# Hymba block on one Trainium2 core: x brought in transposed, first V taken from raw columns, row sums of squares by matmuls with ones

## The chip, the cores and the metric

The kernel runs on one core of one Trainium2 chip. The metric is the device time of one execution in microseconds; the median of several runs is compared. Engines are named as in the profile: PE is TensorE's matmul, PEld its weight load, DVE VectorE, ACT ScalarE, POOL GpSimd, SP the engine that issues most DMAs.

## The reference

One encoder block in fp32 over two requests, a prompt of 512 tokens and a sample of 1024, of width 1024; the kernel treats them as 12 blocks of 128 tokens, or 3 chunks of 512.

```python
xn = rmsnorm(h, norm_mix_g)              # h * rsqrt(mean(h*h) + 1e-6) * g
z = xn @ w_in                            # 3072 columns: q, k, v, g_att, u, g_f of 512 each
att = diff_attention(q, k, v, lam, rel_bias)
att = rmsnorm(att, subln_g, SUBLN_EPS) * (1.0 - lambda_init)
att = att * silu(g_att)
fno = fourier_mix(u, w_f) * silu(g_f)
h = h + concatenate([att, fno]) @ w_out
gate = sigmoid(rmsnorm(h, ple_norm_g) @ w_ple_gate)
h = h + gate * (p_i @ w_ple_proj)
y = rmsnorm(h, final_norm_g)
```

## The kernel before, in words

Every fp32 product is made of three matmuls on two reduced parts: `split` writes a high part (a cast, mostly on ACT, L55) and a low part (source minus high part, mostly on DVE, L59), and `mm3` (L66, L67, L68) adds high*high, high*low and low*high into one PSUM bank. A token block times 512 columns of a weight is 8 k-blocks of three, 24 matmuls.

The stages follow each other on PE:

- **V.** `load_nat(1024)` brings columns 1024 to 1535 of `w_in` in four loads of 512 KB (tile `raw`, pool `pn`, four buffers) and splits them into `wnh`, `wnl`. `prep(t)` takes a block of 128 token rows: Square with a row sum on ACT (L272), mean on DVE, power on POOL (L276), scaled by the row's factor and by `gmix` (the mix weights spread over all partitions) on DVE (L277), eight transposes on PE (L284), and splits into `xh`, `xl`, which hold the normed x transposed, for all later products. `nat(t, wv)` then makes V of the block, and the two parts go to DRAM.
- **k0 and q0.** `blocks(["k0", "q0"])`: the first head's k and q, in transposed form, 24 matmuls (L147) for each of the three chunks and each of the two, 144 in all. Between them `combine(0)` to `combine(2)` work on `w_out`: two loads of 512 KB (tiles `wr`, L324), four subtractions on DVE (L333), splits, four stores to `sot1` to `sot4`. These are the weight sums for a Strassen form of the output product. `load_nat(2048)` for U draws its `raw` tiles from the same four buffers of `pn`.
- **U.** `nat(t, wu)` for 12 blocks, each of 24 matmuls; ACT copies the bank (L354), and the block goes to DRAM. The remaining `combine` calls run beside it.
- **Fourier mixing and attention**, with the other heads' blocks and the Fourier map as filling. Near its end, `all_fill` loads `w_out`, and runs `project(0)` and `project(1)` as filling too: the output product of single blocks, with `keep(t)` (the row goes to `hs` in DRAM, two Squares on ACT, a power on POOL).
- **Project.** `project_pair(t)` for t = 2, 4, .., 10: 7 products of a Strassen form, 12 matmuls each (L528, tiles `bank`), from sums of the four quarter tiles `cl` of two token blocks. For t = 2 the quarters come by `load_cl(2)` and `load_cl(3)` (L541) into two tags of `ph` of two buffers each.
- **Gate.** The gate's weights are loaded, and `gate_pair(t)` does the same form for the gate. `front(t)` loads two rows of `hs` (L861), norms them on ACT (L870), transposes them on PE (L877, 8 to a row) and makes the seven sums; `front(t + 2)` is written ahead of `gate_pair(t)` as one piece, and a list scheduler sets the order on each engine. `per_layer` is the product with `w_ple_proj`; `finish_row` norms the result and stores y.

Each engine, and each DMA queue, takes its instructions in the order that the program was given; SP's queue issues nearly all DMAs, one behind the other, and an issue that waits for a tile holds up the issues behind it. A tile of a tag with n buffers waits until the tile n before it has been read for the last time.

Of the kernel before, what the change touches and what calls it, by code (L numbers as in the profile page):

```python
# [10 lines left out]
F32 = mybir.dt.float32  # L11
F32R = mybir.dt.float32r
AF = mybir.ActivationFunctionType
ALU = mybir.AluOpType
# [18 lines left out]
def block_kernel(ctx, tc, i, yp, ys):  # L33
# [219 lines left out]
    with tc.tile_pool(name="pn", bufs=1, side="right", reuse_waits="tile") as pn:  # L253
        gmix = pn.tile([P, D], F32, name="gmix")

        def load_nat(col):
            wh = pn.tile([P, KB, 512], F32R, tag="wnh", name="wnh", bufs=1)
            wl = pn.tile([P, KB, 512], F32R, tag="wnl", name="wnl", bufs=1)
            for k in range(0, KB, 2):
                raw = pn.tile([P, 2, 512], F32, tag="raw", name="raw", bufs=4)  # L260
                nc.sync.dma_start(out=raw, in_=w_in[:, k:k + 2, col:col + 512])
                split(wh[:, k:k + 2], wl[:, k:k + 2], raw, lo_eng="dve" if k else "pool")
                yield wh, wl

        def load_x(t):
            x = pn.tile([P, D], F32, tag="f4", name="x", bufs=5)
            return x, nc.sync.dma_start(out=x, in_=x_rows(t))

        def prep(t, x):
            xn = pn.tile([P, D], F32, tag="f4", name="xn", bufs=5)  # L270
            ss = pn.tile([P, 2], F32, tag="ss", name="ss", bufs=4)
            sq = nc.scalar.activation(out=xn, in_=x, func=AF.Square, accum_out=ss[:, 0:1])  # L272
            nc.vector.tensor_scalar(out=ss[:, 1:2], in0=ss[:, 0:1], scalar1=1.0 / D,
                                    scalar2=1e-6, op0=ALU.mult, op1=ALU.add)
            rs = pn.tile([P, 1], F32, tag="rs", name="rs", bufs=4)
            nc.gpsimd.tensor_tensor(out=rs, in0=ss[:, 1:2], in1=mhalf[:, 0:1], op=ALU.pow)  # L276
            nc.vector.scalar_tensor_tensor(out=xn, in0=x, scalar=rs, in1=gmix,  # L277
                                           op0=ALU.mult, op1=ALU.mult)
            c, q = t // 4, (t % 4) * P
            for g in range(2):  # L280
                ps = tr()
                for j in range(4):
                    k = g * 4 + j
                    nc.tensor.transpose(out=ps[:, j * P:(j + 1) * P],  # L284
                                        in_=xn[:, k * P:(k + 1) * P], identity=ident)
                ins = split(xh[c][g][:, :, q:q + P], xl[c][g][:, :, q:q + P],
                            ps.rearrange("p (a b) -> p a b", b=P))
            return ins + (sq,)

        x0, _ = load_x(0)  # L290
        nc.scalar.dma_start(out=gmix, in_=i["norm_mix_g"].broadcast_to([P, D]))
        hi0, lo0, sq0 = prep(0, x0)
        wv_parts = load_nat(1024)
        with tc.issue_after(sq0.ins):
            next(wv_parts)
            x1, dma = load_x(1)
            with tc.issue_after(dma.ins), tc.issue_after(hi0.ins), tc.issue_after(lo0.ins):
                prep(1, x1)
                *_, wv = wv_parts
        for t in range(NT):  # L300
            if t == 3:
                with tc.issue_after(hi0.ins):
                    setup(pn)
            if t + 2 < NT:
                prep(t + 2, load_x(t + 2)[0])
            ps = nat(t, wv)
# [3 lines left out]
            split(hi, lo, ps)  # L310
            nc.sync.dma_start(out=vv[s, 0][r:r + P, :], in_=hi.bitcast(F32))
            nc.sync.dma_start(out=vv[s, 1][r:r + P, :], in_=lo.bitcast(F32))

# [773 lines left out]
```

## Time and profile before

| what | value |
|---|---|
| time, median of 3 runs | 958.81 us (957.94 to 960.97) |
| profiled execution | 964.62 us, its span 962.8 us |
| mean granted clock of TensorE | 0.992 |
| PE busy | 915.3 us, 95% of the span |
| DVE / ACT / POOL busy | 66% / 47% / 10% |
| DMA | 175.63 MB, mean 182 GB/s |

The span reaches from the first instruction to the last; the profiled execution's own time lies 1.8 us above it. Busy is the time in which an engine had an instruction in it; matmuls overlap, so a mean duration of one is longer than the distance from one to the next.

### The profile page before, as it was taken

To read this page: it belongs to the slowest core of one execution; us is meant where nothing else is said; L and a number is where in the kernel's file an instruction comes from. 1 tells how busy PE (TensorE), PEld (TensorE's weight loads), DVE (VectorE), ACT (ScalarE), POOL (GpSimd) and SP (SyncE) were. 2 spreads that over 40 slices of the span, in tenths; PEclk is the share of its full clock that TensorE was granted. 3 is DMA by queue.
4 is the path that set the end of the run, shared out by engine and by line. 5 is a ranking of instruction groups with operands and counts; after the bars stand their busy time and mean duration, and the time that the engine had idled before them with its cause. 6 is when DMAs were issued, how large, how long until landed. Compare 5 with 4: busy or idle time off the path is not lost.

```text
span 962.8 us, 13087 instructions
## 1 busy us (share of the span) xinstructions
PE 915.3 (95%) x4536; PEld 747.7 (78%) x4536; DVE 637.5 (66%) x1230; ACT 449.6 (47%) x908; POOL 98.5 (10%) x123
## 2 busy tenths in 40 slices
PE   5999999999999999999999999899899998999995
PEld 4788888888887788888877887777678876777774
DVE  4676443057845698597776978973676777767674
ACT  5543311032324475365554656752343566555542
POOL 3100001010000111000112122421000000000000
PEclk9999999999999999999999999999899999999998
DMA  8669889255547844753577567648875471233211
GB/s 296 226 204 338 290 273 316 85 153 154 164 139 208 228 132 150 202 158 94 180 205 213 166 171 249 195 173 312 290 242 183 143 231 55 93 99 99 93 49 44
DMA packets 123315, 175.63 MB, mean 182 GB/s; under 512 B 9385, under 2 KB 76713, under 8 KB 122225
## 3 DMA queue, kind: packets, MB, share of 16 engines
q1 hardware_dynamic: 121280, 170.72, 55.7%
q0 software_dynamic: 1392, 2.63, 0.9%
q10 hardware_dynamic: 576, 1.44, 0.5%
q8 instruction: 36, 0.59, 0.3%
q14 instruction: 31, 0.25, 0.1%
HBM read 114.96 MB, written 59.80 MB: 182 GB/s over the span
## 4 chain that ended last, share of the span: by engine, by line
PE 72%; DMA 10%; DVE 9%; ACT 4%; issue 2%; SPq 1%; POOL 1%; POOLq 0%; DVEq 0%; ACTq 0%
PE acc L147 23%; PE bank L528 11%; PE sc L657 6%; PE acc L66 6%; PE acc L68 6%; PE acc L67 6%; PE tr L684 3%; DMA x<-hs 2%; DMA raw<-sg 2%; PE tr L67 2%; PE tr L66 2%; PE tr L68 2%; PE tr L414 1%; DMA raw<-w_in 1%; PE tr L284 1%
## 5 line engine op out<-in xcount | busy, mean ns | idle before, releaser
L147 PE MATMUL acc<-xh,wch 128*128 128x512 f32 x384 | 152.2, 396 | 0.0
L147 PE MATMUL acc<-xl,wch 128*128 128x512 f32 x384 | 152.1, 396 | 0.0
L147 PE MATMUL acc<-xh,wcl 128*128 128x512 f32 x384 | 151.7, 395 | 0.0
L663 ACT ACTIVATE pt<-pt,mx 128x1024 f32<-128x1024 f32 (+1 forms) x96 | 96.5, 1007 | 62.4 <-DVE mx L660 61.8
L660 DVE CUSTOM_DVE_ANT_0 pt<-sc,tb 128x1024 f32<-128x1024 f32 (+1 forms) x96 | 97.8, 1041 | 20.3 <-PE sc L657 13.6
L147 PEld LDWEIGHTS acc<-xh,wch 128*128 128x128 f32 x384 | 72.2, 188 | 13.7 <-issue 0.2
L147 PEld LDWEIGHTS acc<-xh,wcl 128*128 128x128 f32 x384 | 72.2, 188 | 13.4
L147 PEld LDWEIGHTS acc<-xl,wch 128*128 128x128 f32 x384 | 72.2, 188 | 13.1 <-issue 0.2
L66 PE MATMUL acc<-wnh,xh 128*128 128x512 f32 x192 | 77.1, 402 | 0.5 <-ACT wnh L55 0.5
L67 PE MATMUL acc<-wnl,xh 128*128 128x512 f32 x192 | 76.8, 400 | 0.0
L68 PE MATMUL acc<-wnh,xl 128*128 128x512 f32 x192 | 76.2, 397 | 0.0
L657 PE MATMUL sc<-kk,qq 128*128 128x512 f32 x160 | 65.7, 411 | 2.4 <-DMA kh_p<-hi 1.6
L657 PE MATMUL sc<-kll,qq 128*128 128x512 f32 x160 | 63.9, 399 | 0.0
L55 ACT CAST wth<-tr 128x512 fp32r<-128x512 f32 x80 | 45.4, 582 | 32.0 <-PE tr L684 31.8
L59 DVE TENSOR_TENSOR wtl<-tr,wth 128x512 fp32r<-128x512 f32 x80 | 53.5, 685 | 6.5 <-ACT wth L55 6.4
L679 DVE SCALAR_TENSOR_TENSOR pt<-pt,rc,pt 128x1024 f32<-128x1024 f32 (+1 forms) x48 | 56.0, 1166 | 1.1
L684 PE MATMUL tr<-ident,pt 128*128 128x128 f32 x320 | 48.4, 276 | 5.8 <-DVE g L729 4.2
L684 PEld LDWEIGHTS tr<-ident,pt 128*128 128x128 f32 x320 | 36.6, 140 | 17.1 <-DVE g L729 6.7
L705 POOL TENSOR_TENSOR g<-ot,g 128x256 f32<-128x256 f32 x24 | 20.3, 847 | 287.6 <-ACT ot L704 282.3
L66 PE MATMUL tr<-wth,v 128*128 128x256 f32 x160 | 45.6, 285 | 0.2 <-DVE wtl L59 0.2
L67 PE MATMUL tr<-wtl,v 128*128 128x256 f32 x160 | 45.5, 284 | 0.3 <-DVE wtl L59 0.2
L68 PE MATMUL tr<-wth,v 128*128 128x256 f32 x160 | 45.1, 282 | 0.0
(297 smaller groups left out, 2056.7 us busy)
## 6 DMA issues: line engine op xcount, KB each, us to landing
raw<-w_in SPq DMA_DIRECT2D x28, 512.0 KB, 5.1
x<-x_sample SPq DMA_DIRECT2D x16, 512.0 KB, 4.7
sot<-o SPq DMA_DIRECT2D x16, 512.0 KB, 4.1
cl<-cT SPq DMA_DIRECT2D x24, 256.0 KB, 3.8
hs<-x SPq DMA_DIRECT2D x12, 512.0 KB, 4.4
x<-hs SPq DMA_DIRECT2D x12, 512.0 KB, 3.8
x<-x_prompt SPq DMA_DIRECT2D x8, 512.0 KB, 5.2
wr<-w_out SPq DMA_DIRECT2D x8, 512.0 KB, 5.8
```

The source lines that it names most:

```text
L55: a = nc.scalar.copy(out=hi, in_=src)
L59: return a, eng.tensor_tensor(out=lo, in0=src, in1=hi.bitcast(F32), op=ALU.subtract)
L66: nc.tensor.matmul(out=out, lhsT=wh, rhs=xh, start=start, stop=False)
L67: nc.tensor.matmul(out=out, lhsT=wh, rhs=xl, start=False, stop=False)
L68: nc.tensor.matmul(out=out, lhsT=wl, rhs=xh, start=False, stop=stop)
L147: nc.tensor.matmul(out=ps, lhsT=a[:, k], rhs=b[c][k // 4][:, k % 4], start=(n == 0), stop=(n == 23))
L528: nc.tensor.matmul(out=out[:, w], lhsT=a[u][:, k], rhs=b[v][:, k, w], start=(start and k == 0 and n == 0), stop=(k == 3 and n == 2), skip_ ...
L657: nc.tensor.matmul(out=pss[c][:, n:n + 512], lhsT=qq[c], rhs=k[c][:, n:n + 512], start=(m == 0), stop=(m == 1))
L660: nc.vector.tensor_tensor_reduce(out=pt[c][:, :T], in0=ps[:, :T], in1=tb[:, off:off + T], scale=-1.0, scalar=3e38, op0=ALU.add, op1=ALU.mi ...
L663: nc.scalar.activation(out=pt[c][:, :T], in_=pt[c][:, :T], func=AF.Exp, scale=-1.0, bias=mx[:, c:c + 1], accum_out=sm[:, c:c + 1])
L679: nc.vector.scalar_tensor_tensor(out=pt[0][:, :T], in0=pt[1][:, :T], scalar=rc[:, 1:2], in1=pt[0][:, :T], op0=ALU.mult, op1=ALU.add)
L684: nc.tensor.transpose(out=ps[:, j * P:(j + 1) * P], in_=pt[0][:, (b + j) * P:(b + j + 1) * P], identity=ident)
```

## The change

It has three parts. **Front:** the host hands x over transposed (`x_cols`, three chunks of 1024 by 512) and the mix weights as columns (`mix_cols`). The transposes of x and the spread `gmix` are gone. V of chunk 0 is made from raw columns times the mix weight, k-block by k-block, for four token blocks at once in four half banks; the row factor is applied when the banks are read out (`values_out`). Row sums of squares come from Squares on ACT, added over the k-blocks on DVE (`square`), and from matmuls of that sum with a matrix of ones (`stats`); `across` spreads the row factors over the partitions by transposes, and `normed_in` norms a chunk. Chunk 0's columns are loaded a second time and normed after V. **Places:** tiles `raw` of `load_nat` and `wr` of `combine` now come from `px`, where `load_col` has its own, two buffers for all, instead of four buffers of `pn`; the first weights are loaded from ACT's queue. **Project and gate:** block 3's quarters are loaded into a tile of their own (`whole`), `keep` of block 1 waits until the first pair's sums are made, and both rows are loaded ahead. The gate's `front` is a generator in four parts, stepped inside `gate_pair`: loads at its start, the first row's transposes ahead of product s2*t2, the second's ahead of s3*t3, the sums at the end. The order of the products with t2 and with 22 is as before; the sums s2 and s4 swap.

```diff
-        gmix = pn.tile([P, D], F32, name="gmix")
+        gm = pn.tile([P, KB], F32, name="gm")
...
+        def weights_in(wh, wl, k, col, queue=None):
+            raw = px.tile([P, 2, 512], F32, tag="raw", name="raw", bufs=2)
+            if queue:
+                for m in range(2):
+                    queue.dma_start(out=raw[:, m], in_=w_in[:, k + m, col:col + 512])
+                    split(wh[:, k + m], wl[:, k + m], raw[:, m])
+            else:
+                nc.sync.dma_start(out=raw, in_=w_in[:, k:k + 2, col:col + 512])
+                split(wh[:, k:k + 2], wl[:, k:k + 2], raw)
...
         def load_nat(col):
-            wh = pn.tile([P, KB, 512], F32R, tag="wnh", name="wnh", bufs=1)
-            wl = pn.tile([P, KB, 512], F32R, tag="wnl", name="wnl", bufs=1)
+            w = nat_tiles()
             for k in range(0, KB, 2):
-                raw = pn.tile([P, 2, 512], F32, tag="raw", name="raw", bufs=4)
-                nc.sync.dma_start(out=raw, in_=w_in[:, k:k + 2, col:col + 512])
-                split(wh[:, k:k + 2], wl[:, k:k + 2], raw, lo_eng="dve" if k else "pool")
-                yield wh, wl
...
+                weights_in(*w, k, col)
+            return w
...
+        def square(total, x, k):
+            if k == 0:
+                nc.scalar.activation(out=total, in_=x[0][:, 0], func=AF.Square)
+                return
+            sq = pn.tile([P, 512], F32, tag="sq", name="sq", bufs=2)
+            nc.scalar.activation(out=sq, in_=x[k // 4][:, k % 4], func=AF.Square)
+            nc.vector.tensor_tensor(out=total, in0=total, in1=sq, op=ALU.add)
...
+        def stats(total):
...
+            split(th[:, 0:4], tl[:, 0:4], total.rearrange("p (a b) -> p a b", b=P))
+            ps = tr()
+            for t in range(4):
+                for n, x in enumerate((th, tl)):
+                    nc.tensor.matmul(out=ps[:, t * P:(t + 1) * P], lhsT=x[:, t], rhs=ones,
+                                     start=(n == 0), stop=(n == 1))
+            rs = pn.tile([P, 4], F32, tag="rs", name="rs", bufs=3)
+            nc.vector.tensor_scalar(out=rs, in0=ps.rearrange("p (a b) -> p a b", b=P)[:, :, 0],
+                                    scalar1=1.0 / D, scalar2=1e-6, op0=ALU.mult, op1=ALU.add)
+            nc.gpsimd.tensor_tensor(out=rs, in0=rs, in1=mhalf, op=ALU.pow)
+            return rs
...
+        def normed_in(x, c, rt):
+            for k in range(KB):
+                v = x[k // 4][:, k % 4]
+                nc.vector.scalar_tensor_tensor(out=v, in0=v, scalar=gm[:, k:k + 1], in1=rt,
+                                               op0=ALU.mult, op1=ALU.mult)
+                split(xh[c][k // 4][:, k % 4], xl[c][k // 4][:, k % 4], v)
...
+        ts, ps = range(4), sc_pair() + sc_pair()
+        for k in range(6):
+            v_part(ts, ps, k)
+        rs0 = stats(total)
+        x1, total = squares(1)
+        for k in range(6, KB):
+            v_part(ts, ps, k)
+        for t in ts:
+            values_out(t, ps[t], rs0[:, t:t + 1])
+        normed_in(x1, 1, across(stats(total)))
...
+        normed_in(x0, 0, across(rs0))
...
             for j in range(2):
-                r.append(pn.tile([P, 2, 512], F32, tag="raw", name="wr", bufs=4))
+                r.append(px.tile([P, 2, 512], F32, tag="raw", name="wr", bufs=2))
...
-        *_, wu = load_nat(2048)
+        wu = load_nat(2048)
...
-        for t in range(2):
-            yield from project(t, early[t], load_x(t))
-            if t == 0:
-                for n in ("t4", "t1"):
-                    load_sums(n)
-            pair_cl.extend(load_cl(t + 2))
-            yield
-        x2.append(load_x(2))
+        rows = [load_x(t) for t in range(2)]
+        yield from project(0, early[0], rows[0])
+        for n in ("t4", "t1"):
+            load_sums(n)
+        pair_cl.extend(load_cl(2))
+        whole = wo.tile([P, KB, P], F32, tag="x", name="c3", bufs=3)
+        nc.sync.dma_start(out=whole, in_=cT[0].rearrange("(k p) t -> p k t", p=P)[:, :, 3 * P:4 * P])
+        pair_cl.extend([whole[:, 0:4], whole[:, 4:8]])
+        yield
+        yield from project(1, early[1], rows[1], False)
...
+        a = left(pair_cl)
+        keep(*later[0])
...
         def gate_pair(t, x, p, g, a):
+            ahead = front(t + 2) if t + 2 < NT else iter(())
+            next(ahead, None)
...
             pp = per_layer(p[0], 1)
+            next(ahead, None)
             product(b0, a["s2"], wb["t2"], False)
...
             pp = per_layer(p[1], 1)
+            next(ahead, None)
             product(b0, a["s3"], wb["t3"], False)
```

The scheduler's order moves with it. On PE, the program before begins like this (`tr` a bank of transposes, `acc` a block's bank; the number at a row's start is its place):

```order
1 L284 MATMUL tr<-ident,xn 128x128 x8
2 L66 MATMUL acc<-wnh,xh_170 128x512
3 L67 MATMUL acc<-wnl,xh_170 128x512
4 L68 MATMUL acc<-wnh,xl_176 128x512
5 L66 MATMUL acc<-wnh,xh_170 128x512
6 L67 MATMUL acc<-wnl,xh_170 128x512
7 L68 MATMUL acc<-wnh,xl_176 128x512
8 L66 MATMUL acc<-wnh,xh_170 128x512
9 L284 MATMUL tr<-ident,xn 128x128 x8
```

In the changed program PE begins at once with V of chunk 0 in banks `sc`, and between chunk 0's last matmul and chunk 1's first there stand the eight small matmuls with ones (of chunk 1's squares) and the four transposes that spread its row factors:

```order
104 L68 MATMUL sc<-wnh,xl_177 128x512
105 L304 MATMUL tr<-ones,th 128x128
106 L304 MATMUL tr<-ones,tl 128x128
107 L304 MATMUL tr<-ones,th 128x128
108 L304 MATMUL tr<-ones,tl 128x128
109 L304 MATMUL tr<-ones,th 128x128
110 L304 MATMUL tr<-ones,tl 128x128
111 L304 MATMUL tr<-ones,th 128x128
112 L304 MATMUL tr<-ones,tl 128x128
113 L316 MATMUL tr<-ident,rs 128x128 x4
114 L66 MATMUL acc<-wnh,xh_172 128x512
115 L67 MATMUL acc<-wnl,xh_172 128x512
```

So the transposes of x are gone, and chunk 1's matmuls stand behind that chunk's whole statistics.

On SP's queue, the loads of U's weights (`raw_1168`, `raw_1172`, `raw_1176`, `raw_1180`) stand in the program before among the stores of k0's parts (`kh`, `kl`):

```order
65 L261 DMA raw_1168<-w_in 128x2x512
66 L179 DMA kh_p00_67<-hi_918 64x512
67 L180 DMA kh_p01_69<-hi_918 64x512
68 L181 DMA kl_p0_70<-lo_919 128x512
69 L261 DMA raw_1172<-w_in 128x2x512
70 L261 DMA raw_1176<-w_in 128x2x512
71 L179 DMA kh_s00_98<-hi_950 64x512
72 L180 DMA kh_s01_100<-hi_950 64x512
73 L181 DMA kl_s0_101<-lo_951 128x512
74 L261 DMA raw_1180<-w_in 128x2x512
75 L324 DMA wr_1212<-w_out 128x1024
76 L324 DMA wr_1214<-w_out 128x1024
```

In the changed program they stand here, behind the stores of q0's last chunk (`hi_1098`, `lo_1099`), behind `wr_1108`, which is the second load of `combine(2)`, and among its stores `sot1` to `sot4`:

```order
73 L166 DMA qs_s00_97<-hi_1098 64x512
74 L167 DMA qs_s01_99<-hi_1098 64x512
75 L168 DMA qs_s00_97<-lo_1099 64x512
76 L169 DMA qs_s01_99<-lo_1099 64x512
77 L417 DMA wr_1108<-w_out 128x1024
78 L435 DMA sot1_144<-o_1115 256x1x512
79 L265 DMA raw_1131<-w_in 128x2x512
80 L435 DMA sot2_145<-o_1115 256x1x512
81 L435 DMA sot3_146<-o_1122 256x1x512
82 L435 DMA sot4_147<-o_1122 256x1x512
83 L265 DMA raw_1135<-w_in 128x2x512
84 L265 DMA raw_1139<-w_in 128x2x512
```

They moved past the rest of k0, all of q0 and `combine(2)`: `raw_1131` has the buffer that `wr_1106`, combine's first load, had. On PE, U's first matmul follows q0's last at once in both.

In the gate, the second row's eight transposes for the next pair (`raw` the normed row) stood before inside the product with 22, here in the first pair:

```order
3595 L528 MATMUL bank<-w22h,ahs_7665 128x512
3596 L528 MATMUL bank<-w22l,ahs_7665 128x512
3597 L877 MATMUL tr<-ident,raw 128x128 x8
3598 L528 MATMUL bank<-w22h,als_7666 128x512
3599 L66 MATMUL acc<-wp0h,ph 128x512
3600 L67 MATMUL acc<-wp0l,ph 128x512
3601 L68 MATMUL acc<-wp0h,pl 128x512
3602 L66 MATMUL acc<-wp1h,ph 128x512
3603 L67 MATMUL acc<-wp1l,ph 128x512
3604 L68 MATMUL acc<-wp1h,pl 128x512
```

In the changed program they stand behind that product and behind the six matmuls of `per_layer` (`wp0`, `wp1`):

```order
3601 L622 MATMUL bank<-w22l,ahs_7680 128x512
3602 L622 MATMUL bank<-w22h,als_7681 128x512
3603 L66 MATMUL acc<-wp0h,ph 128x512
3604 L67 MATMUL acc<-wp0l,ph 128x512
3605 L68 MATMUL acc<-wp0h,pl 128x512
3606 L66 MATMUL acc<-wp1h,ph 128x512
3607 L67 MATMUL acc<-wp1l,ph 128x512
3608 L68 MATMUL acc<-wp1h,pl 128x512
3609 L989 MATMUL tr<-ident,raw 128x128 x8
3610 L622 MATMUL bank<-wt3h,ahs_7676 128x512
3611 L622 MATMUL bank<-wt3l,ahs_7676 128x512
```

They moved back by seven matmuls here.

## Rows read from the trace of the kernel before

**Rows 1.** The page, part 4: the chain that ended last, share by engine.

```profile
PE 72%; DMA 10%; DVE 9%; ACT 4%; issue 2%; SPq 1%; POOL 1%; POOLq 0%; DVEq 0%; ACTq 0%
```

**Rows 2.** Timeline, 0 to 13 us: start, duration, engine, line, tiles, shape, count, [idle before].

```profile
5.85 1.06 ACT L272 ACTIVATE xn<-x 128x1024 f32<-128x1024 f32 x1 [3.16 <-DMA x<-x_prompt]
...
7.27 0.57 POOL L276 TENSOR_TENSOR rs<-ss,mhalf 128x1 f32<-128x1 f32 x1 [4.48 <-DVE ss L273]
...
9.21 1.97 PE L284 MATMUL tr<-ident,xn 128*128 128x128 f32 x8 [9.21 <-DVE xn L277]
10.37 0.58 ACT L55 CAST xh<-tr 128x512 fp32r<-128x512 f32 x1 [1.28 <-PE tr L284]
...
11.01 0.79 PE L66 MATMUL acc<-wnh,xh 128*128 128x512 f32 x1
```

**Rows 3.** Groups of PE instructions, 0 to 95 us: busy us, mean ns, then idle before.

```profile
L66 PE MATMUL acc<-wnh,xh 128*128 128x512 f32 x96 | 39.1, 409 | 0.5 <-ACT wnh L55 0.5
...
L284 PE MATMUL tr<-ident,xn 128*128 128x128 f32 x96 | 13.9, 288 | 10.9 <-DVE xn L277 10.6 <-DVE xl L59 0.3
```

**Rows 4.** Timeline of ACT, 126 to 146 us.

```profile
127.00 1.05 ACT L55 CAST wch<-raw 128x1024 fp32r<-128x1024 f32 x1 [4.61 <-PE acc L147]
127.96 0.59 ACT L163 ACTIVATE hi<-acc 128x512 fp32r<-128x512 f32 x1
132.85 0.59 ACT L354 COPY u<-acc 128x512 f32<-128x512 f32 x1 [4.30 <-PE acc L68]
138.47 0.59 ACT L354 COPY u<-acc 128x512 f32<-128x512 f32 x1 [5.04 <-PE acc L68]
```

**Rows 5.** Timeline of SP's DMA queue, 86 to 146 us.

```profile
97.66 0.62 SPq L261 DMA_DIRECT2D raw<-w_in  x1
...
107.85 0.45 SPq L261 DMA_DIRECT2D raw<-w_in  x1
...
130.43 0.60 SPq L169 DMA_DIRECT2D qs_s<-lo  x1
...
133.83 1.41 SPq L324 DMA_DIRECT2D wr<-w_ple_gate  x3
```

**Rows 6.** Timeline of DVE, 126 to 146 us.

```profile
129.23 0.68 DVE L164 SCALAR_TENSOR_TENSOR lo<-acc,hi 128x512 fp32r<-128x512 f32 x1
137.51 0.75 DVE L326 TENSOR_SCALAR wr<-wr,gcol 128x1024 f32<-128x1024 f32 x1 [7.59 <-DMA wr<-w_ple_gate]
138.29 0.69 DVE L333 TENSOR_TENSOR f<-wr,f 128x512 f32<-128x512 f32 x1
```

**Rows 7.** The page, part 6: DMA issues, KB each, median us to landing.

```profile
raw<-w_in SPq DMA_DIRECT2D x28, 512.0 KB, 5.1
...
wr<-w_out SPq DMA_DIRECT2D x8, 512.0 KB, 5.8
```

**Rows 8.** Timeline of PE, 668 to 692 us.

```profile
672.58 0.49 PE L528 MATMUL bank<-w21h,ah 128*128 128x512 f32 x1 [1.82 <-ACT ah L55]
...
685.38 0.63 PE L528 MATMUL bank<-w11h,ah 128*128 128x512 f32 x1
...
687.94 0.49 PE L528 MATMUL bank<-wt4h,al 128*128 128x512 f32 x1
```

**Rows 9.** Windows: PE, PEld, DVE, ACT, POOL busy (x instructions), PE clock, DMA share, GB/s.

```profile
680.00:690.00 10.00, 8.76 (x25) 6.49 (x26) 7.31 (x12) 4.89 (x7) 0.00 (x0) 0.66 0.58 212
850.00:860.00 10.00, 8.06 (x40) 6.53 (x40) 5.03 (x8) 5.52 (x10) 0.32 (x1) 0.94 0.36 120
860.00:870.00 10.00, 10.00 (x42) 8.17 (x41) 7.17 (x11) 4.39 (x8) 0.00 (x0) 0.89 0.00 0
```

**Rows 10.** What PE waited for, 812 to 950 us: us in total, times, longest.

```profile
PE tr L877 <- ACT raw L870: 3.6, 4, 1.9
PE acc L66 <- DVE raw L919: 0.8, 2, 0.5
```

**Rows 11.** Timeline of PE, 855 to 864 us.

```profile
858.74 1.96 PE L877 MATMUL tr<-ident,raw 128*128 128x128 f32 x8 [1.94 <-ACT raw L870]
```

More of the change, by code (lines that the diff above doesn't have):

```diff
@@ L265, in load_x @@
[L265 to L288, printed above, removed]
@@ L309, in block_kernel, with v_part @@
             lo = ph.tile([P, 512], F32R, tag="lo", name="lo", bufs=2)
-            split(hi, lo, ps)
+            if rs is None:
+                split(hi, lo, ps)
+            else:
+                nc.scalar.mul(out=hi, in_=ps, mul=rs)
+                nc.vector.scalar_tensor_tensor(out=lo, in0=ps, scalar=rs, in1=hi.bitcast(F32),
+                                               op0=ALU.mult, op1=ALU.subtract)
             nc.sync.dma_start(out=vv[s, 0][r:r + P, :], in_=hi.bitcast(F32))
             nc.sync.dma_start(out=vv[s, 1][r:r + P, :], in_=lo.bitcast(F32))
+        def v_part(ts, ps, k):
+            for t, bank in zip(ts, ps):
+                c, q = t // 4, (t % 4) * P
+                a, b = (x[c][k // 4][:, k % 4, q:q + P] for x in (xh, xl))
+                mm3(bank, a, b, wv[0][:, k], wv[1][:, k], k == 0, k == KB - 1)
@@ new lines, in sc_pair @@
+        def sc_pair():
+            both = sc()
+            return [both[:, 0:512], both[:, 512:1024]]
+        x0, total = x_tiles(), total_tile()
+        wv = nat_tiles()
+        for k in range(KB):
+            if k < 2:
+                x_in(x0, 0, k, 1)
+            elif k % 2 == 0:
+                x_in(x0, 0, k, 2)
+            if k % 2 == 0:
+                weights_in(*wv, k, 1024, None if k else nc.scalar)
+            v, h = x0[k // 4][:, k % 4], xh[0][k // 4][:, k % 4]
+            nc.scalar.mul(out=h, in_=v, mul=gm[:, k:k + 1])
+            nc.vector.scalar_tensor_tensor(out=xl[0][k // 4][:, k % 4], in0=v, scalar=gm[:, k:k + 1],
+                                           in1=h.bitcast(F32), op0=ALU.mult, op1=ALU.subtract)
+            square(total, x0, k)
@@ new lines, in block_kernel, with squares @@
+        full = px.tile([P, P], F32, tag="th", name="full", bufs=3)
+        nc.vector.memset(full, 1.0)
+        nc.scalar.copy(out=ones, in_=full)
+        def squares(c):
+            x, total = x_tiles(), total_tile()
+            for k in range(0, KB, 2):
+                x_in(x, c, k, 2)
+            for k in range(KB):
+                square(total, x, k)
+            return x, total
+        ts, ps = range(4), sc_pair() + sc_pair()
+        for k in range(6):
+            v_part(ts, ps, k)
@@ new lines, in block_kernel @@
+        rs0 = stats(total)
[5 more added lines that the diff above has]
+        normed_in(x1, 1, across(stats(total)))
+        x2, total = squares(2)
+        x0 = x_tiles()
+        for k in range(0, KB, 2):
+            x_in(x0, 0, k, 2)
+        rt2 = None
+        for n, ts in enumerate(((4, 5), (6, 7), (8, 9), (10, 11))):
+            if n == 2:
+                normed_in(x2, 2, rt2)
+            ps = sc_pair() if n % 2 else [acc(), acc()]
+            for k in range(KB):
+                v_part(ts, ps, k)
+            for t, bank in zip(ts, ps):
+                values_out(t, bank)
+            if n == 0:
+                rt2 = across(stats(total))
+            if n == 1:
+                setup(pn)
@@ L567, in keep, with project @@
         rpow(rs, rs)
[L569 removed]
+    def project(t, cl, x, now=True):
         ch = [wo.tile([P, 4, P], F32R, tag="tmp", name="ch", bufs=2) for _ in range(2)]
@@ L583, in project @@
             nc.vector.tensor_tensor(out=x[:, w], in0=x[:, w], in1=ps[z], op=ALU.add)
-        keep(t, x)
+        if now:
+            keep(t, x)
+        else:
+            later.append((t, x))
     def all_fill():
@@ L988, in gate_pair @@
             finish_row(t, 1, x, g, ss, 3 if last else 2)
-        first = [rows_in(t) for t in range(2)]
+            return next(ahead, None)
+        first = front(0)
+        next(first)
         for n, tag in (("11", "x*00"), ("21", "x*10"), ("t4", "t4*"), ("t1", "t1*"), ("t2", "x*01"),
@@ L994, in block_kernel @@
             if n == "t1":
-                nxt = front(0, first)
+                *_, nxt = first
             w = wblock(n, tag)
```

105 lines of the change are left out of this document (61 added, 44 removed).

## The prediction

> **What bounds the kernel now.** I read the page first: PE is busy for 95% of the span, and the chain that ended last lies on PE for 72% and on DMA for 10% [rows 1]. So a change pays by removing PE work, or idle time of PE, and costs by adding either. Then I read PE stage by stage. From the timeline of the start: PE does nothing before 9.21, because the first x must land (ACT's Square starts at 5.85), go through power on POOL and be scaled on DVE; the first matmul of V starts at 11.01 [rows 2]. The groups of the first 95 us show 96 transposes of x with 13.9 us [rows 3]. Around U, ACT reads q0's last bank at 127.96, U's first bank at 132.85 and its second at 138.47 [rows 4]: 24 matmuls take 5.62 us, 0.234 each, and PE goes from q0 to U without a wait, since U's weights were asked for at 97.66 to 107.85, twenty microseconds earlier [rows 5]. At the start of the project stage PE waits 1.82 us and then more, and runs slowly [rows 8, 9]. In the gate it waits 3.6 and 0.8 us in all [rows 10].
>
> **Front.** Before: q0 ends at about 127.9 [rows 4]; its and k0's 144 matmuls are 33.7 us, so V ends at 94.2. V's 83.2 us from 11.0 are 288 matmuls (67.4), the transposes after the first eight (13.9 - 1.97 = 11.9) [rows 2, 3] and 3.9 of bias products and waits.
> After: the first x block and the first weight block are 256 KB, half of what ACT waited for until 5.85, so I take 4.9 for their landing, add a cast of 0.58 [rows 2] and some for the low part on DVE: first matmul at 5.8 (bounds 5 and 7). Then 288 matmuls (67.4); 24 small matmuls with ones and 12 spreading transposes, bounded by 0 and by the transposes' own 11.9/88 = 0.135 each, taken at the latter (4.9); bias products and small waits 1.9 (half of 3.9); a start at the low clock 1.3, since the first rows here are slow too (1.97 for eight transposes where the others average 1.08; 0.79 for a matmul) [rows 2]. New waits: chunk 1's first matmul stands behind its whole statistics. A mean on DVE (0.15, as small operations there), power 0.57 [rows 2], norming 0.68 as the 128x512 form [rows 6] and a cast 0.59 make 2.0, with the hops between engines 2.3. Chunk 2's statistics lie beside chunk 1's matmuls. Ahead of k0, chunk 0 is normed again: its first block's norming and cast, 1.4. In k0, chunk 0's and 2's banks now end together, and the next bank waits for a read-out and low part: 0.59 + 0.68, 1.4 with hops. For ACT and DVE that alternate in chunk 0, 0.9. All in all 5.8 + 67.4 + 4.9 + 1.9 + 1.3 + 2.3 + 1.4 + 1.4 + 0.9 = 87.3, plus 33.7: q0 ends at 121.0, **6.9 us earlier** (4 to 8.5). The Squares (ACT, 8 of 0.55 to a chunk, half of the 1.06 of a 1024-wide one [rows 2]), their sums and the norming (DVE, per k-block about 0.6 + 0.68 + 0.6 = 1.9) hide behind 12 matmuls to a k-block (2.8); without that cover a chunk would cost 8 x 1.9 - a few us.
>
> **U's weights.** This is the largest term, and it is a loss. Call q0's end T (127.9 before). The first load of U's weights has the buffer that combine(2)'s first load had, whose last reader is combine's third subtraction, and that needs combine's second load. This one stands on SP behind the stores of q0's last chunk. So nothing of it can start before T. In the trace's own rows: the bank's high part starts at T + 0.1 [rows 4], its low part at T + 1.3 [rows 6], and the last of the four stores is issued by 131.03, T + 3.1 [rows 5]. combine's load then is issued; one issued at 133.83 had landed when DVE started on it at 137.51 [rows 5, 6], 3.7 us, so T + 6.8 (with the median 5.8 of this kind [rows 7], T + 8.9). Second and third subtraction, about 0.6 each by their spacing and 0.69 to the end [rows 6]: T + 8.1. The first U load, 3.7 to 5.1 [rows 6, 7], taken at 4: T + 12.1. Its cast 1.05 [rows 4]: U's first matmul at T + 13.2, not T. The second load is behind the stores `sot2` to `sot4`, issued when their splits are done (about T + 12), and lands at T + 17.2 with 5.1. The third waits for the first to be split, the fourth for the second: T + 17.2 + 1.05 + 1.2 (low part) = 19.5, + 4 = 23.5, + 2.2 = 25.7. Then the last pair's matmuls, 12 x 0.234, not all of them behind the low part: the first two blocks of U, together 48 matmuls, end at about T + 28.2, where without a wait they end at T + 11.2. **Cost 17 us.** From below: 11.5, if combine's and U's first load take 3 us and the rest come right behind; from above 21, with medians everywhere. Nothing else is in PE's queue there; the later blocks of U are not held up, and the work behind U stays in order.
>
> In that wait PE's clock may drop. In the trace PE ran at a mean granted clock of 0.66 between 680 and 690, after idle times of 1.82 us and more, with 6 matmuls from 685.38 to 687.94, 0.427 each, the 1.2 GHz level [rows 8, 9]. Twelve matmuls at that level are 5.1 us, about one load's distance, so only the last pair's show: 2.3 at most, which I leave to the upper bound. The Trainium skill ("TensorE: Matmul & The Clock Gate", section "HAM oscillation — how this bites in real kernels") says that a loop whose every K-tile waits for its DMA starts each tile at the low clock, which speaks against a U stage fed pair by pair; by it the loss would be 19 and not 17. The trace agrees in kind with its 0.66.
>
> **Project.** Before, PE's wait of 1.82 us ends at 672.58; from its start at 670.76 to 687.94, 32 matmuls start, 7.5 us of work in 17.2: 9.7 lost [rows 8]. After: block 3's quarters no longer wait for tiles of `ph`. Two additions of 0.69, the first Square beside the second, two Squares of 0.6 and a cast of 0.59 give a first bank at 3.1, and about 11 matmuls run; four more casts, two sums and a low part give 7.4, then the other 21 run densely: 12.3, so 4.8 lost. Gain 4.9, less 0.3 for some low clock: **4.6** (2 to 6).
>
> **Gate.** Lost before: 3.6 + 0.8 [rows 10], and 1.7 of low clock (means of 0.94 and 0.89 in two windows of 10 us [rows 9], where eight transposes take 1.96 [rows 11]). After, the second row's transposes come behind the product with 22 and `per_layer`, 1.6 us and more later, and both rows are asked for at the pair's start. I leave 1.5: the 0.8 behind DVE and 0.7 for `per_layer` behind tiles that DVE frees. **Gain 4.6** (2 to 6).
>
> **Sum.** -6.9 + 17 - 4.6 - 4.6 = +0.9 against the profiled 964.62; that run stood 5.8 above the median of 958.81, so the median moves to **959.7**. What a measurement of this kernel can tell from no change is about 0.3%, 2.9 us: no measurable change.
>
> **Rivals.** (1) Faster, by a cheap wait: if transfers in the quiet around T land in 3 us and U's other three loads come right behind the first, the cost is 11.5, and the time 954.2. For it: the 3.7 above is a whole interval from issue to use, in which the clock of other queues ran too. Against: two loads wait for splits, which no faster transfer removes. It decides below a cost of 13. (2) Slower, by the pair-wise feeding: loads at medians of 5.1 and 5.8 behind four stores, and the last pairs at 0.427: cost 21 to 22, time 964.2. For it: the page's medians [rows 7]; it decides above 19. (3) The project and gate stages keep half of their waits (the casts stand behind the Squares of block 1 on ACT; `per_layer` behind DVE): +4.6, time 964.3. (4) The front gains only 4, as chunk boundaries open twice (chunk 2's norming late on DVE): time 962.6. (5) The scheduler's place for U's loads costs nothing since PE has other work: no, q0's last matmul is followed by U's first.
>
> **Chances.** Forecast (within 0.3%) 0.36; rival 1 (with a front or gate at the good end) 0.28; rival 2 0.20; rival 3 0.11; rival 4 0.05. So faster 0.28, same 0.36, slower 0.36. The terms' bounds, taken as independent (2.2, 4, 2 and 2), give 5.4, and 8 in 10 reaches 7 to each side: 952.5 to 967; the forecast alone 956 to 961.7.
>
> **What would show it.** Right: PE's first matmul at 5 to 7; q0's last at 119.5 to 124; a PE wait of about 13 for `wnh` right behind it, with U's `raw` loads issued after q0's last stores; the first two blocks of U ready about 28 us after q0; no wait over 1 us in the middle of the gate; at project's start about 5 lost. Wrong: U's first bank within 20 us of q0's last, or chunk boundaries of V with waits over 5, or a clock well under 0.9 through all of U.

## The result

The changed kernel takes 969.12 us (median of 4 runs, 966.85 to 973.03) against 958.55: a ratio of 1.0106, 95% interval 1.0084 to 1.0129. It is slower by 10.6 us, or 1.1%; the forecast was 959.7, no measurable change, with a range to 967. Its profiled execution took 966.85 us, 2.2 more than before's profiled 964.62, which stood high; so the two profiles show a smaller difference than the runs.

Where it went, stage by stage in the two profiles: q0's last matmul starts at 126.81 before and 127.14 after, so the front gained nothing. U's last bank is copied at 194.74 before and 211.97 after, 17.2 later. The project stage's first product comes at 672.58 and 689.39, still 16.8 later. The gate's last product comes at 954.09 and 956.24, 2.2 later. The rows of the first two, each time before and then after:

```profile
126.81 0.39 PE L147 MATMUL acc<-xh,wcl 128*128 128x512 f32 x1
...
194.74 0.59 ACT L354 COPY u<-acc 128x512 f32<-128x512 f32 x1 [5.04 <-PE acc L68]
```

```profile
127.14 0.39 PE L147 MATMUL acc<-xh,wcl 128*128 128x512 f32 x1
...
211.97 0.59 ACT L448 COPY u<-acc 128x512 f32<-128x512 f32 x1 [0.75 <-PE acc L68]
```

The page after, part 4 and the row of part 5 with the largest waits of a matmul, which answer to [rows 1]:

```profile
PE 75%; DVE 10%; DMA 6%; ACT 4%; issue 2%; POOL 1%; SPq 1%; POOLq 0%; DVEq 0%; ACTq 0%
...
L66 PE MATMUL acc<-wnh,xh 128*128 128x512 f32 x128 | 51.3, 406 | 15.2 <-ACT wnh L55 13.7
```

PE's share of that chain grew, and L66 waited 15.2 us where it had waited 0.5 in all before. What PE waited for in the first 200 us (us in total, times, longest):

```profile
PE acc L66 <- ACT wnh L55: 13.7, 2, 12.7
PE tr L316 <- POOL rs L309: 7.0, 2, 5.8
PE sc L66 <- ACT xh L362: 5.8, 1, 5.8
PE acc L66 <- ACT xh L55: 1.5, 1, 1.5
PE acc L147 <- ACT xh L55: 1.5, 1, 1.5
PE acc L147 <- DVE lo L59: 1.4, 1, 1.4
```

The first is U's wait; the second is mostly one wait of 5.8 between chunk 0 and chunk 1 of V, and 1.2 more in chunk 1, for chunk 2's statistics; the third is the start, where the first matmul starts at 5.77, as forecast (5.8) against 11.01 in [rows 2].

**U.** ACT after, at q0's last read-out, U's first cast and its first two banks, and SP's loads, which answer to [rows 4] and [rows 5]:

```profile
127.56 0.60 ACT L163 ACTIVATE hi<-acc 128x512 fp32r<-128x512 f32 x1 [4.84 <-PE acc L147]
...
139.08 1.04 ACT L55 CAST wnh<-raw 128x1024 fp32r<-128x1024 f32 x1 [2.43 <-DMA raw<-w_in]
...
155.84 0.59 ACT L448 COPY u<-acc 128x512 f32<-128x512 f32 x1 [0.20 <-PE acc L68]
156.99 0.59 ACT L448 COPY u<-acc 128x512 f32<-128x512 f32 x1 [0.56 <-PE acc L68]
```

```profile
130.59 0.58 SPq L417 DMA_DIRECT2D wr<-w_out  x1
...
135.43 0.39 SPq L265 DMA_DIRECT2D raw<-w_in  x1
...
138.65 10.09 SPq L265 DMA_DIRECT2D raw<-w_in  x3
```

q0 ends at 127.4. combine's second load is issued 3.2 us later, U's first at 135.4, the other three (one row, from 138.65) as their tiles come free. PE waits 12.66 us, and the two first banks are ready 28.4 and 29.6 us after q0: the chain and the size that the prediction worked out (28.2). PE at U's first two pairs of k-blocks:

```profile
140.18 1.22 PE L66 MATMUL acc<-wnh,xh 128*128 128x512 f32 x2 [12.66 <-ACT wnh L55]
...
145.44 0.63 PE L68 MATMUL acc<-wnh,xl 128*128 128x512 f32 x1
147.13 0.74 PE L66 MATMUL acc<-wnh,xh 128*128 128x512 f32 x2 [1.05 <-ACT wnh L55]
...
148.97 0.40 PE L66 MATMUL acc<-wnh,xh 128*128 128x512 f32 x1
```

**Front.** DVE, POOL and PE between chunk 0 and chunk 1:

```profile
33.02 0.74 DVE L335 SCALAR_TENSOR_TENSOR lo<-sc,rs,hi 128x512 fp32r<-128x512 f32 x1
33.69 1.48 DVE L291 TENSOR_TENSOR total<-total,sq 128x512 f32<-128x512 f32 x2
35.08 0.75 DVE L335 SCALAR_TENSOR_TENSOR lo<-sc,rs,hi 128x512 fp32r<-128x512 f32 x1
35.74 0.15 DVE L307 TENSOR_SCALAR rs<-tr 128x4 f32<-128x4 f32 x1
```

```profile
35.97 1.40 POOL L309 TENSOR_TENSOR rs<-rs,mhalf 128x4 f32<-128x4 f32 x1 [6.25 <-DVE rs L307]
```

```profile
31.35 0.28 PE L304 MATMUL tr<-ones,tl 128*128 128x128 f32 x1
37.42 1.11 PE L316 MATMUL tr<-ident,rs 128*128 128x128 f32 x4 [5.80 <-POOL rs L309]
40.03 0.80 PE L66 MATMUL acc<-wnh,xh 128*128 128x512 f32 x1 [1.49 <-ACT xh L55]
40.62 0.63 PE L67 MATMUL acc<-wnl,xh 128*128 128x512 f32 x1
```

The matmuls with ones of chunk 1 end at 31.6. The mean that they feed runs on DVE only at 35.74: chunk 2's sums of squares and chunk 0's low parts stand ahead of it. The power then takes 1.40 us for 128x4, where the 128x1 of [rows 2] took 0.57. After 5.8 us of waiting the transposes take 1.11 for four, and chunk 1's first matmul comes at 40.03, and slow (0.63 and more). The gap is counted here and below from the end of the last matmul with ones (31.63) to this matmul: 8.4 us. The granted clock of these windows, which answer to [rows 9]:

```profile
30.00:40.00 10.00, 2.74 (x16) 2.08 (x14) 7.67 (x14) 6.56 (x12) 1.40 (x1) 0.68 0.48 185
134.00:160.00 26.00, 18.16 (x63) 12.95 (x64) 12.44 (x17) 9.61 (x13) 0.00 (x0) 0.76 0.70 234
```

**Project and gate.** PE's waits from 668 us to the end, which answer to [rows 10] and to the waits in [rows 8]:

```profile
PE bank L622 <- ACT ah L55: 2.8, 1, 2.8
PE bank L622 <- DVE raw L899: 1.7, 1, 1.7
PE tr L989 <- ACT c L1002: 0.9, 1, 0.9
...
PE tr L989 <- ACT raw L982: 0.7, 1, 0.7
```

Before, the wait on the normed rows (`raw`) in the whole gate was 7.0 us, 3.4 of it near 803 and 3.6 from 812 on [rows 10]; now it is 0.7:

```profile
PE tr L877 <- ACT raw L870: 7.0, 5, 3.4
```

The 7 products of the first pair begin after one wait of 2.78 us, and their first matmuls then come 0.43 to 0.63 us apart, up to 695.90:

```profile
689.39 0.80 PE L622 MATMUL bank<-w21h,ah 128*128 128x512 f32 x1 [2.78 <-ACT ah L55]
...
695.90 0.39 PE L622 MATMUL bank<-w11h,cl 128*128 128x512 f32 x1
```

### The profile page after: what moved, and what is told of

Read it like the earlier page. It is cut to its first block, busy times and chain, and to the rows that moved or that the text cites. A ratio compares the mean times of both kernels' runs of the same rounds, so it can differ in the third digit from the quotient of the medians.

```text
span 965.0 us, 12989 instructions
## 1 busy us (share of the span) xinstructions
PE 908.5 (94%) x4476; PEld 744.0 (77%) x4476; DVE 658.7 (68%) x1269; ACT 461.8 (48%) x921; POOL 94.0 (10%) x112
## 4 chain that ended last, share of the span: by engine, by line
PE 75%; DVE 10%; DMA 6%; ACT 4%; issue 2%; POOL 1%; SPq 1%; POOLq 0%; DVEq 0%; ACTq 0%
PE acc L147 24%; PE bank L622 16%; PE sc L756 6%; PE acc L66 4%; PE acc L67 4%; PE acc L68 4%; PE tr L783 3%; DMA raw<-w_in 3%; PE tr L67 2%; PE tr L66 2%; PE tr L68 2%; DMA raw<-sg 1%; DVE total L291 1%; PE tr L508 1%; PE sc L67 1%
## 5 line engine op out<-in xcount | busy, mean ns | idle before, releaser
L66 PE MATMUL acc<-wnh,xh 128*128 128x512 f32 x128 | 51.3, 406 | 15.2 <-ACT wnh L55 13.7
L67 PE MATMUL acc<-wnl,xh 128*128 128x512 f32 x128 | 52.0, 407 | 0.6 <-DVE wnl L59 0.5
L68 PE MATMUL acc<-wnh,xl 128*128 128x512 f32 x128 | 51.2, 404 | 0.0
L783 PEld LDWEIGHTS tr<-ident,pt 128*128 128x128 f32 x320 | 36.6, 140 | 17.2 <-DVE g L828 6.3
L804 POOL TENSOR_TENSOR g<-ot,g 128x256 f32<-128x256 f32 x24 | 20.3, 846 | 289.9 <-ACT ot L803 284.2
L66 PE MATMUL tr<-wth,v 128*128 128x256 f32 x160 | 45.6, 285 | 0.2 <-DVE wtl L59 0.2
```

What stands on the lines that cost most here:

```text
L66: nc.tensor.matmul(out=out, lhsT=wh, rhs=xh, start=start, stop=False)
L67: nc.tensor.matmul(out=out, lhsT=wh, rhs=xl, start=False, stop=False)
L68: nc.tensor.matmul(out=out, lhsT=wl, rhs=xh, start=False, stop=stop)
L783: nc.tensor.transpose(out=ps[:, j * P:(j + 1) * P], in_=pt[0][:, (b + j) * P:(b + j + 1) * P], identity=ident)
```

## The experiments

The times of one group were measured on the same chip beside runs of the kernel before, whose median stands with them; times of different groups are best compared by these ratios.

**1. U's loads ahead of combine(2)** (changed kernel).

```diff
             if n % 2:
                 combine(n // 2)
+            if n == 3:
+                wu = load_nat(2048)
         run(first)
-        wu = load_nat(2048)
```

> The changed kernel, with load_nat(2048) written after combine(1) and so ahead of combine(2): U's weight loads no longer wait for combine(2)'s tiles. If the wait between q0 and U is the loss (its two first blocks ended 28.3 to 29.4 us after q0 where 11.2 would do), U starts at once and the time falls by 14 to 17 us, to 952 to 955. Rival: the kernel lost elsewhere (lower clock, the later stages in runs without a profile), and the time falls by less than 5, to 964 or more.

Measured: 965.93 us against 959.82 (ratio 1.0066, 1.0047 to 1.0085), only 3.2 below the changed kernel. U's long wait is gone (the longest is 1.3, and U's last copy is at 198.25, not 211.97), and a new one stands behind U. PE's longest wait from 195 to 300 us, and SP's queue there:

```profile
PE acc L147 <- ACT wch L55: 9.0, 1, 9.0
```

```profile
190.65 1.94 SPq L417 DMA_DIRECT2D wr<-w_ple_gate  x2
...
202.27 0.93 SPq L126 DMA_DIRECT2D raw<-w_in  x1
```

The same load in the kernel before:

```profile
162.00 1.34 SPq L126 DMA_DIRECT2D raw<-w_in  x2
```

k1's weights (`load_col`) draw on the same two buffers as U's weights and `combine`; in the kernel before they were asked for at 162.00, here at 202.27, behind the last `combine`. So the loss is not one late load but the two buffers that everything goes through. Neither expectation's mechanism was right; the time is the rival's.

**2. Chunk 2's Squares behind chunk 1's norming** (changed kernel).

```diff
-                split(xh[c][k // 4][:, k % 4], xl[c][k // 4][:, k % 4], v)
+                last = split(xh[c][k // 4][:, k % 4], xl[c][k // 4][:, k % 4], v)
+            return last
...
-        normed_in(x1, 1, across(stats(total)))
-        x2, total = squares(2)
+        hi1, lo1 = normed_in(x1, 1, across(stats(total)))
+        with tc.issue_after(hi1.ins), tc.issue_after(lo1.ins):
+            x2, total = squares(2)
```

> The changed kernel, with chunk 2's Squares and their sums on ACT and DVE queued behind chunk 1's norming. If the wait of 5.8 us ahead of the spreading transposes comes from DVE's queue (the mean of chunk 1 stood behind chunk 2's sums, 4.1 us after the matmuls with ones), the gap between chunk 0's and chunk 1's matmuls falls from 8.4 to about 4.5 us and the time by 4 to 6 us, to 963 to 965. Rival: the chain through power, transposes, norming and cast is that long by itself; the gap stays over 7 and the time within 1.5 us of 969.

Measured: 969.43 us against 959.82 (1.009, 1.006 to 1.012). The gap shrank from 8.4 to 5.3 us and q0's last matmul starts at 124.77, 2.4 earlier, but U's last copy is at 211.53, only 0.4 earlier: from q0's last matmul to the copy of U's first bank it took 30.6 us and not 28.7. So DVE's order as a cause of the gap is shown, and a gain in time is not: what is won ahead of U is lost there. In this kernel the mean still stands behind two read-outs on DVE:

```profile
32.06 0.75 DVE L336 SCALAR_TENSOR_TENSOR lo<-sc,rs,hi 128x512 fp32r<-128x512 f32 x1 [0.28 <-ACT hi L335]
33.57 0.75 DVE L336 SCALAR_TENSOR_TENSOR lo<-sc,rs,hi 128x512 fp32r<-128x512 f32 x1 [0.76 <-ACT hi L335]
34.23 0.15 DVE L307 TENSOR_SCALAR rs<-tr 128x4 f32<-128x4 f32 x1
```

**3. Project and gate parts alone, on the kernel before.**

> The kernel before with the project and gate parts of the change alone. If these stages gained what the two profiles show from project(1) to the end (283.4 and 269.8 us, 13.6), the time is 945 to 947; by the sum of the prediction, 9.2, it is 949.4. Rival: the profiled run of before had longer waits there than its other runs, and the gain is 3 to 6, 953 to 956; or the early part's delay is what made room for it, and there is none.

Measured: 954.54 us against 959.82 (0.995, 0.9929 to 0.9971). The gain is 5.3 us, as the first rival said, and not 9.2 or 13.6.

**4. Front and places alone, on the kernel before.**

> The kernel before with the front and the places of the change alone. If the profiles are right (q0's end 0.4 us earlier, 17 us lost at U, about 1 given back in the attention), the time is 958.6 + 16 = 974 to 976. By the prediction (6.9 gained, 17 lost) it would be 968.7. Rival: with the later stages as before, part of the 17 is given back where PE waited for DMAs there, and the time is under 966.

Measured: 978.77 us against 959.82 (1.0192, 1.0149 to 1.0235), so 19 us lost by the front and the places, where the prediction's sum says 10.1. q0's last matmul starts at 129.09 here, and U's last copy is at 215.07, 20.3 later than before. In the gate, whose code is that of before, PE waited for normed rows 1.0 us, where the first profile of before shows 7.0:

```profile
PE tr L971 <- ACT raw L964: 1.0, 3, 0.6
```

**5. The kernel before once more.**

> The kernel before, once more, for a second profile. If the 7.0 us that PE waited for normed rows in the gate of the first profile belong to that one execution (its time stood 5.8 us above the median), this profile shows under 3 us of them, and its time is 957 to 961. If they belong to the kernel, they are there again, 6 to 8 us.

Measured: 962.86 us, its profiled execution; the median of the runs beside it is 958.81. So the profiled execution of before stood high again, by 4 us, and the wait is there, at 4.4 us, most of it one of 4.0 near 803 and 0.5 from 812 on:

```profile
PE tr L877 <- ACT raw L870: 4.4, 3, 4.0
```

Neither expectation holds: both profiles of before show the wait near 803, and its size and the waits behind it changed.

**6. The project part alone, on the kernel before.**

> The kernel before with the project part of the change alone (block 3's quarters in a tile of their own, rows ahead, the deferred keep; the gate as before). Project and gate together gave 5 us. If the project part gave what its rows show (3.9 us for the first three products), this one gives 3 to 4.5 and the gate 0.5 to 2: time 955 to 956.5. Rival: the gate part gave most of it, and this one is within 1.5 us of before.

Measured: 955.21 us against 958.81 (0.9946, 0.9921 to 0.9971). It gains what both parts gained together. In its gate, unchanged, the wait for normed rows is smaller too:

```profile
PE tr L888 <- ACT raw L881: 2.5, 3, 2.0
```

**7. U's loads ahead, and combine's loads in a tile of pn** (changed kernel; with the edit of experiment 1).

```diff
-            r = []
+            both = pn.tile([P, 4, 512], F32, tag="xs", name="wr", bufs=4)
+            r = [both[:, 0:2], both[:, 2:4]]
             for j in range(2):
-                r.append(px.tile([P, 2, 512], F32, tag="raw", name="wr", bufs=2))
```

> The changed kernel with load_nat(2048) ahead of combine(2), and combine's loads in a tile of the pool pn that stands free by then, instead of the two buffers shared with all weights. If the two shared buffers are what kept the first experiment from paying (PE then waited 9.0 us after U for k1's weights, whose load stood behind combine's), both waits go: U's last copy near 198, no wait over 2 us behind it, time 950 to 954. Rival: the transfers themselves are late (DMA or SP's queue), a wait of 5 or more stays behind U, and the time is 960 or more.

Measured: 953.51 us against 958.81 (0.9947, 0.9922 to 0.9972), 15.6 below the changed kernel. U's first and last copy:

```profile
134.14 0.59 ACT L449 COPY u<-acc 128x512 f32<-128x512 f32 x1 [2.30 <-PE acc L68]
...
194.61 0.59 ACT L449 COPY u<-acc 128x512 f32<-128x512 f32 x1 [4.91 <-PE acc L68]
```

Behind U PE waits 1.5 us at most. So the whole of U's loss comes back when the buffers and the order are both undone. The ratio is that of the project and gate parts alone (0.995 in experiment 3, 0.9947 in 12): with the front added nothing more is gained in time.

**8. The same with chunk 2's Squares late** (edits of 2 and 7).

> The seventh experiment with the second one's order as well (chunk 2's Squares behind chunk 1's norming), which moved q0's end 2.4 us earlier, and was lost again at U. If that loss was U's wait on combine's tiles, it now stays: 2 to 3 us under the seventh, 948 to 951. Rival: it is given back elsewhere again, and the two are within 1 us.

Measured: 953.72 us against 958.81 (0.9934, 0.9906 to 0.9963), the same as the seventh within their spread (945.44 to 957.83). U's last copy is at 192.39, 2.2 earlier, but the project stage's first product at 674.73 against 674.37: given back between, and where in those 480 us was not found.

**9. Combine's loads in pn, U's loads at their place** (changed kernel with the edit of 7 alone).

> The changed kernel with combine's loads in a tile of pn alone, load_nat(2048) at its place behind combine(2). If the shared buffers are the larger part of the loss and the order in the program the smaller, two of U's four loads now run early, no wait for k1's weights is left behind U, and a wait of 4 to 7 us stays in U for the third and fourth load, which still stand on SP behind combine's stores: U's last copy at 199 to 202, time 956 to 960. Rival: without the order nothing comes early, U starts as late as before (last copy over 208), time 964 or more.

Measured: 962.39 us against 960.45 (1.0018, 1.0006 to 1.003). PE's longest wait for U's weights:

```profile
PE acc L66 <- ACT wnh L55: 8.1, 1, 8.1
```

The wait for k1's weights is gone, but U's last copy is at 209.00, not 199 to 202: two loads came early, the other two stood behind combine's stores on SP, and U's first bank was ready at 150.39. In part this profile is late from further ahead: q0's last matmul starts at 131.06, 3.9 later than in the changed kernel, with longer stretches at the low clock (granted 0.96 where the changed kernel had 1.00, between 90 and 130 us). From that matmul to U's last copy it took 77.9 us, against 84.8 in the changed kernel and 66.4 in the seventh experiment. With the order alone 3.2 us of time came back, with the buffers alone 6.7, with both 15.6 (3.8, 8.4 and 15.2 by the ratios). That each holds back what the other frees is shown by the waits that stay, 9.0 and 8.1; that both together give more than the sum of the two is not clear of the intervals.

**10. The mean first** (edits of 7 and 2, and chunk 0's read-out behind chunk 1's norming).

```diff
-        for t in ts:
-            values_out(t, ps[t], rs0[:, t:t + 1])
         hi1, lo1 = normed_in(x1, 1, across(stats(total)))
         with tc.issue_after(hi1.ins), tc.issue_after(lo1.ins):
+            for t in ts:
+                values_out(t, ps[t], rs0[:, t:t + 1])
             x2, total = squares(2)
```

> The eighth experiment with chunk 0's read-out written behind chunk 1's norming too, so that chunk 1's mean stands on DVE right behind the matmuls with ones. If DVE's queue made the gap (in the second experiment the mean still stood 1.6 us behind read-outs), the spreading transposes follow the last matmul with ones by about 2 us (power 1.0 to 1.4), chunk 1 starts 1 to 2 us earlier than in the second experiment, and q0 ends at 122.5 to 124. In time: 1 to 2 us under the eighth, 951 to 953, if what is won in the front is kept; equal to it, if the attention gives it back as it did there.

Measured: 950.48 us against 960.45 (0.9908, 0.988 to 0.9937). DVE, POOL and PE at the same place:

```profile
32.83 0.16 DVE L307 TENSOR_SCALAR rs<-tr 128x4 f32<-128x4 f32 x1 [1.09 <-PE tr L304]
```

```profile
33.07 1.02 POOL L309 TENSOR_TENSOR rs<-rs,mhalf 128x4 f32<-128x4 f32 x1 [1.80 <-DVE rs L307]
```

```profile
32.52 0.27 PE L304 MATMUL tr<-ones,tl 128*128 128x128 f32 x1
34.15 0.65 PE L316 MATMUL tr<-ident,rs 128*128 128x128 f32 x4 [1.35 <-POOL rs L309]
36.29 0.80 PE L66 MATMUL acc<-wnh,xh 128*128 128x512 f32 x1 [1.49 <-ACT xh L55]
```

The mean follows the matmuls with ones at once, the transposes run at 0.65, and the gap is 3.5 us. q0's last matmul starts at 123.59 and U's last bank is copied at 190.31. Even so q0 ends at 123.8, 2.8 us later than the forecast. This version beats the kernel before by 0.9% and the changed kernel by nearly 2%; against the eighth (0.9934, 0.9906 to 0.9963) the gain is not clear of the intervals.

**11. The gate part alone, on the kernel before.**

> The kernel before with the gate part of the change alone. Project and gate together gave 0.5% and the project part alone 0.5%, so the gate part should give nothing: within 1.5 us of before. The same gate code has shown waits for normed rows of 7.0, 4.4, 2.5 and 1.0 us in four executions, so what it saves is small in most. Rival: it gains 2 to 5 us by itself, as the prediction's 4.6 said, and the two parts do not add up.

Measured: 955.28 us against 960.5 (0.9948, 0.9928 to 0.9967). The rival was right: it gains 5 us by itself, as much as the project part does and as both did together in experiment 3.

**12. The third once more, with more runs.**

> The third experiment's kernel (project and gate parts on the kernel before) once more, with more rounds, since the parts alone gave 0.53% and 0.52% and both together 0.50%. If they add up, the ratio is 0.989 to 0.991 and the third experiment was a low draw; if they share a wait (the one of 3.4 to 4.0 us near 803 in both profiles of before, of 2.0 with the project part alone and gone with the gate part), it is 0.994 to 0.996 again.

Measured: 953.12 us against 958.26 (0.9947, 0.9928 to 0.9965), as in the third. The sum of the single gains would be 0.989, so the two parts do not add up.

## Why the prediction was wrong

The sum said +0.9 us and the runs +10.6. The front, forecast at -6.9, gained nothing, and that is most of the miss; the project and gate parts, forecast at -9.2, gave about -5; U's loss was right.

**U's weights (+17): right.** The chain, its place (behind q0's last chunk and combine(2)) and its size: 28.4 and 29.6 us to the first two banks against the forecast 28.2, 17.2 later at U's last copy, and 15.6 us of time back in experiment 7. What it did not say is that the two shared buffers hold back k1's weights too; the late U hid that (experiment 1).

**Low clock in U's wait (0 to 2.3, not charged): right in kind.** Between 134 and 160 us the granted clock was 0.76. After the wait of 12.66 twelve matmuls came 0.43 us apart or more, from 140.18 on, the 1.2 GHz level, and the second pair of k-blocks ran at full speed a matmul or two after its own waits of 1.05 and 0.52 us. The Trainium skill ("TensorE: Matmul & The Clock Gate", section "HAM oscillation — how this bites in real kernels") has every K-tile start at the low clock in a loop that waits 3 to 5 us for its DMA at each; here only the first wait was that long, and only its pair started low.

**Front (-6.9): the step that failed.** Measured no gain: q0's last matmul starts at 126.81 before, 127.14 after and 129.09 in experiment 4, which has the same front. In timed runs the front and the places cost 19.0 us (experiment 4) where the sum says 10.1, and with U's loss undone nothing is left of the front's gain (experiment 7). One of the prediction's own signs of being wrong came, a wait over 5 at a chunk boundary of V (5.8). Terms of its sum were mis-sized, or left at nothing:

- "A mean on DVE, power 0.57, norming and a cast make 2.0, with hops 2.3": with the transposes, about 0.5 of what the sum had apart, the gap was 8.4 us. The mean stood behind whatever the scheduler had put on DVE ahead of it, and the power of four columns takes 1.0 to 1.55. Experiments 2 and 10 show the queue: 8.4, 5.3 and 3.5 us as the sums and then the read-outs move behind the mean.
- DVE's load was taken as hidden by counting its time per k-block; what mattered was its order. So chunk 2's statistics, which the sum had as hidden, made PE wait 1.2 us too.
- The low clock, 1.3 in the sum: the first nine matmuls, from 5.77 to 9.78, took 1.9 us more than at their later distance of 0.229, and chunk 1's first nine, from 40.03 to 44.00, 1.9 more again.
- The sum was made against 127.9, where ACT began to read q0's last bank; but ACT was then at a cast of 1.05 until about 128 [rows 4], and q0 ended at 127.0, so 0.9 of the gain was never there.

Against these stand some 2.4 us by which the matmuls were cheaper than the 0.234 of the sum (0.229 in V, 0.227 in k0 and q0). What stood: the start (5.77), the waits ahead of and in k0 (1.49 and 1.45, forecast 1.4 each).

**Project (-4.6): right in time, less sure in the profiles.** From the end of project(1) to the first product of t1 for t = 4 the profiles show 38.7 us in both of before, 33.7 after and 33.5 with the project part alone: 5 us. But 2 of the 5 also went where the project code is that of before (36.6 in experiment 11, 36.3 in 4). Inside the sum, the 0.3 for low clock was too small: the first 14 matmuls of the changed kernel's first pair, from 689.39 to 695.90, took 3.3 us more than at 0.23. In time the part alone gives 0.54%.

**Gate (-4.6): right alone, wrong in the sum.** Alone it gives 0.52%; added to the project part nothing more. My gate term looked for the gain in the waits from 812 on [rows 10], which in the second profile of before are 1.4 us, and took the wait near 803, where the norming on ACT stands behind casts of late weight loads, as unchanged. PE waits there 3.4 us in the first profile of before, 4.0 in the second, 2.0 with the project part, 0.7 with the gate part, and 1.6 and none in the two profiles with both on the kernel before. That the two parts share this wait, and so do not add up, is argued and not shown: in experiment 4, which has neither part, it is 0.6. What the profiles do show is where the project part's gain goes: with both parts (experiments 3 and 12) it is 2.1 and 3.3 us less than with the gate part alone up to the first product of t1 for t = 4, and 2.2 and 2.5 more from there to the last product. Why, no run shows.

**The offset.** I carried a difference of profiles over to the median unchanged. Before's profiled executions stood 4 to 6 us above its median both times; of the others the ninth experiment's stood 3.9 above and the rest within 2.3 us of theirs (966.85 of 969.12, 954.17 of 954.54, 955.73 of 955.21). From project(1)'s end to the last product the profiles of before took 283.3 and 281.5 us, those of the kernel before with either part or both 271.5 to 272.5: a gain of 9 to 12 that is 5 in the timed runs. Experiment 4, whose late stages are those of before, took 275.5. So a part of what the late stages seemed to offer was in the profiled executions of before alone. Why a profile costs this kernel more, no run shows; that its loads are slower then is an argument only.

With these: front 0 to +2, U +16, late stages -5, together +11 to +13, against 10.6 measured. Rival 2 (slower by U's loads) gave the right side for the wrong size; rival 4 (the front gains less) named the true place with too small a chance. Experiment 4 and the changed kernel differ by 9.7 us (978.77 and 969.12, in different groups), more than the 5 of the late parts. Of the 10.4 between their profiled executions 4.5 arise ahead of project(1)'s end, 3.1 of them by U's last copy, where the two have the same program text; so this is not a gain of the late parts alone, and its cause stays open.

## What to carry to other kernels

A pool of two buffers shared by several streams of loads is one queue: list everything that draws on it in order, and price the last one, not only the first to wait. A short chain across engines (matmul, mean, power, transpose, norm, cast) is as long as the queue on each engine when its link arrives, so read the order of the changed program at each link, not the operations' durations alone. And when the profiled execution stands above the median, do not carry gains read from its waits over to the median: here 9 to 12 us of them were 5 in the timed runs.

## What the runs showed of the hardware

- The power on POOL took 0.55 to 0.57 us for 128x1 in the front of the kernel before, 0.54 to 0.86 in the gate of the changed kernel, and 1.01 to 1.55 for 128x4.
- Four transposes of 128x128 took 0.65 us, and 1.11 after an idle time of 2.7 to 6.2 us. The next matmuls then came 0.42 to 0.59 us apart, eight of them in the second experiment and 13 in the ninth. In the tenth, twelve did so behind transposes that took 0.65, after waits of 1.35 and 1.49.
- From 5 to 10 us of the changed kernel the profile's clock reads 1.00, though the matmuls there came 0.43 us apart, as they did between 40 and 44, where it reads 0.51.
- U's banks came every 5.62 us before [rows 4] and every 5.50 in the changed kernel, with the same 24 matmuls each at the full clock; why is not known. Over U's ten later blocks that is 1.2 us.
